# A hybrid encoder block on one core: more down-projection pairs by seven products, block sums through GpSimd's queue, and weights tiled on the host

## The chip, the cores and the metric

The kernel runs on one core of a Trainium2 chip. The metric is the device time of one execution in microseconds. TensorE is called PE, VectorE DVE, ScalarE ACT, GpSimd POOL and SyncE SP, as in the profile; a DMA's queue is called by the engine that issues it.

## What is computed

One layer of an encoder on 256 tokens of width 2048, all in float32. The reference, cut to its main lines:

```python
hn = rmsnorm(h, mix_norm_pre)
z, xbc, dt_raw, u = split(hn @ w_in)            # 2048 -> 1024 + 1536 + 32 + 1024
y_ssd = ssd_mixer(z, xbc, dt_raw, ...)          # bidirectional state-space mixer
y_pool = pool_mixer(u, pool_w, pool_scale)
h = h + rmsnorm(concat([y_ssd, y_pool]) @ w_out, mix_norm_post)
hn = rmsnorm(h, ffn_norm_pre)
gate, val = split(hn @ w_up)                    # 2048 -> 2 x 5632
ff = (gelu(dwconv_centred(gate, conv_w, conv_b)) * val) @ w_down    # 5632 -> 2048
h = h + rmsnorm(ff, ffn_norm_post)
gate = sigmoid(rmsnorm(h, ple_norm_pre) @ w_ple_gate)
h = h + rmsnorm(gate * (p @ w_ple), ple_norm_post)
```

## The kernel before

The work is a row of matmul stages on PE: "dtu" and "xbc" and "z" (parts of `w_in`), "wo" (`w_out`), "up" (`w_ffn_up`), "down" (`w_ffn_down`, names with `dn`), "ple" and "gate" (names with `gt`). Weights come from HBM into a tile called raw (three buffers of 128 x 2048 floats, 1 MiB each). A float32 product is made of three products of a shorter form: `split` (L141) lets ACT round a weight to its high part (L152) and DVE take the difference as its low part (L153), and PE adds high x high, high x low and low x high. High and low parts have five buffers each. Everything else that is large lies in 13 "pages" of 1 MiB, and intermediate results in three "mid" tiles of half that size.

**Up** (L874 to L895) goes through 11 slabs of 512 gate and 512 value columns. A slab has four calls of `feature_pairs` (L340) with two pieces each, so up has 88 pieces; a piece uses one raw tile of 8 blocks of 128 rows by 256 columns. After a slab's gate, DVE and ACT do the convolution and the gelu, POOL multiplies by `rfb`, the tokens' norm factor (L885), and after each half of the values DVE writes the activations `hid` into pages (L895). At the end of each piece `aside` (L196) runs the jobs that stand in the list `work` for that piece.

**Down** (L954, through `sublayer` and `token_major`) makes its 2048 columns in two halves of 1024. Each half goes over the 44 blocks of `hid` in 22 pairs of blocks, numbered 0 to 21. A plain pair is 2 blocks x 2 token tiles x 2 column blocks x 3 = 24 matmuls of 512 columns. A fast pair treats the 2 x 2 blocks of weights and activations by seven products instead of eight, 21 matmuls (`seven_products`, L239), and needs sums of the weights' four blocks and of the activations' four blocks. `combine` (L269) puts the products together at the end of the fast pairs of a half.

- The sums of weights are made during up by jobs of `block_sums` (L208): fetch the pair's 1 MiB into a page, add on DVE two pieces later (`add_blocks`, L232), and in the piece after that store the page to a tile in HBM. Down then loads this page again (`dn..t`) and, of the original weights, three of the four blocks (L245, L246). The last two pairs of the list are held in their pages. All these DMAs stand in SP's queue.
- The sums of activations are made in down by `pair_sums` (L773, L777 to L782), on DVE and ACT. For four of the fast pairs they are kept in two pages from the first half for the second (`dn_keep`).

The instructions are put in order per engine by a scheduler that takes those that are ready in the order of the program. `tc.issue_after(i)` puts the instructions of a block that are issued on `i`'s engine behind `i`; `load` (L116) uses it to put a DMA on SP's queue behind the last weight load.

At pair 13 of the second half the residual `h` is loaded back into two pages (`back`, L937), and at pair 16 `first_gate` (L943) prepares the gate's first pair: a load, two passes by ACT over 128 x 2048 (L948, L950) and an accumulating DMA issued by POOL (L949), which makes the low part.

In z, the mixer's output y is summed by POOL and DVE (`skip` L672, `mix` L676).

Of the kernel before, what the change touches and what calls it, by code (L numbers as in the profile page):

```python
# [11 lines left out]
F32 = mybir.dt.float32  # L12
F32R = mybir.dt.float32r
AF = mybir.ActivationFunctionType
ALU = mybir.AluOpType
# [36 lines left out]
def build(nc, a, out):  # L52
    x = a["x"][0]
    w_in, w_out, w_up = a["w_in"][0], a["w_out"][0], a["w_ffn_up"][0]
    w_down, w_gate, w_ple = a["w_ffn_down"][0], a["w_ple_gate"][0], a["w_ple"][0]
    out = out[0]

    with tile.TileContext(nc) as tc, \
# [37 lines left out]
        c_dt = DSSD + 1536  # L96
        r0 = wp.tile([P, 2048], F32, tag="raw", bufs=3, name="dtur0")
        for n in range(2):
            first = ins(nc.scalar.dma_start(r0[:, n * 352:(n + 1) * 352],
                                            w_in[:P, c_dt + n * 352:c_dt + (n + 1) * 352]))  # L100
# [15 lines left out]
        def load(dst, src, ahead=False):  # L116

            with tc.issue_after(last["dma"]) if last and not ahead else nullcontext():
                return ins(nc.sync.dma_start(dst, src))

# [35 lines left out]
        def raw(name, src, a_, b_):  # L156
            r = wp.tile([P, 2048], F32, tag="raw", bufs=3, name=name)
            if src is None:
                return r
            last["dma"] = load(r[:, :a_ * b_].rearrange("p (a b) -> p a b", a=a_), src, True)  # L160
            return r
# [46 lines left out]
        def block_sums(name, w, c0, k, held):  # L208
# [15 lines left out]
            def store():  # L224
                if not held:
                    t = dp.tile([P, 2048], F32, tag=f"{name}s{c0}_{k}", bufs=1, name=f"{name}s{c0}_{k}")
                    load(t, pg[0])
                    sums_[name, c0, k] = t, False

            return [fetch], [], [add], [store]  # L230

        def add_blocks(r):  # L232

            v = r.rearrange("p (b c) -> p b c", b=4)
            nc.vector.tensor_add(v[:, 0:2], v[:, 0:2], v[:, 1::2])  # L235
            nc.vector.tensor_add(v[:, 3], v[:, 3], v[:, 0])
            nc.vector.tensor_add(v[:, 2], v[:, 2], v[:, 3])

        def seven_products(name, stage, w, k0, c0, a_, acc, alt, start, stop):  # L239
# [3 lines left out]
            if (stage, c0, k0) in sums_:  # L243
                r = raw(f"{name}r", None, 0, 0)
                last["dma"] = load(r[:, 512:1536], w[(k0 + 1) * P:(k0 + 2) * P, c0:c0 + 1024], True)  # L245
                last["dma"] = load(r[:, :512], w[k0 * P:(k0 + 1) * P, c0:c0 + 512], True)  # L246
# [4 lines left out]
                b11 = split(f"{name}a", r[:, :512], 512)  # L251
                b2 = split(f"{name}b", r[:, 512:1536], 1024)
            else:
                r = t = raw(f"{name}r", w[k0 * P:(k0 + 2) * P, c0:c0 + 1024]
                            .rearrange("(k p) c -> p k c", p=P), 2, 1024)
                b11 = split(f"{name}a", r[:, :512], 512)
                b2 = split(f"{name}b", r[:, 1024:], 1024)
# [33 lines left out]
        def token_major(name, w, c0, ks, get, acc, tail=1, fast=(), alt=None, sums=None, at=()):  # L291
# [3 lines left out]
            for u in range(nu):  # L295
# [3 lines left out]
                if u in fast:  # L299
                    if u == fast[0]:  # L300
# [3 lines left out]
                r = None if f"{name}{k0}_0" in ready else raw(f"{name}r{k0}", w[k0 * P:(k0 + 2) * P, c0:c0 + 1024]  # L304
                                                               .rearrange("(k p) c -> p k c", p=P), 2, 1024)
# [8 lines left out]
                for t, (o, c), (k, wh, wl), q in order:  # L314
                    xh, xl = (v[:, t * P:(t + 1) * P] for v in get(k))
                    xx, ww = ((xh, wh), (xh, wl), (xl, wh))[q]
                    mm(o, xx, ww[:, c:c + o.shape[-1]], k == ks[0] and q == 0, k == ks[-1] and q == 2)
# [5 lines left out]
        def feature_major(name, w, c0, get, acc):  # L323

            for u in range(4):
                r = raw(f"{name}r{u}", w[u * 512:(u + 1) * 512, c0:c0 + 512]
                        .rearrange("(k p) c -> p k c", p=P), 4, 512)
# [12 lines left out]
        def feature_pairs(name, w, c0, get, acc):  # L340


            for u in range(2):
                r = raw(f"{name}r{u}", w[u * 1024:(u + 1) * 1024, c0:c0 + 256]
                        .rearrange("(k p) c -> p k c", p=P), 8, 256)
# [97 lines left out]
        for u in range(0, NK, 2):  # L443
            r = [wp.tile([P, 2048], F32, tag="raw", bufs=3, name=f"dtur{u}") if u else r0, page(f"dtur{u + 1}")]
            for j in range(2):
                k = u + j
                if k == 0:
                    last["dma"] = load(r[0][:, 704:1056], w_in[:P, c_dt + 704:c_dt + 1056])
# [3 lines left out]
                for c0, c1 in ((0, 704), (704, 1056)) if k == 1 else ((0, 1056),):  # L452
                    last["dma"] = load(r[j][:, c0:c1], w_in[k * P:(k + 1) * P, c_dt + c0:c_dt + c1])
# [29 lines left out]
        with tc.issue_after(half[0]), tc.issue_after(half[1]):  # L483
# [11 lines left out]
            for a_ in range(4):  # L495
# [17 lines left out]
        load(pmat.rearrange("p (g s t) -> p g s t", g=4, s=2),  # L513
             a["pool_matrix"].rearrange("g (s p) t -> p g s t", p=P))
        poolw = page("poolw")
        load(poolw.rearrange("p (g c d) -> p g c d", g=4, c=2),
             a["pool_w"][0].rearrange("g (c p) d -> p g c d", p=P))
# [122 lines left out]
        def xbc(slab):  # L640
            acc = main(f"xbc{slab}")
            feature_major(f"xb{slab}", w_in, DSSD + slab * 512, hn, acc)
# [29 lines left out]
        def skip(t):  # L672
            nc.gpsimd.tensor_tensor(by_head(y[:, t * 1024:(t + 1) * 1024]), by_head(xs[:, t * 1024:(t + 1) * 1024]),
                                    dsk.unsqueeze(2).to_broadcast([P, H, 64]), op=ALU.mult)

        def mix(t, g):  # L676
# [8 lines left out]
            nc.gpsimd.tensor_add(y[:, c0:c0 + 512], y[:, c0:c0 + 512], tm)  # L685
# [45 lines left out]
        token_major("z", w_in, 0, list(range(NK)), hn, zacc)  # L731
# [42 lines left out]
        def pair_sums(name, s, o, a11, a21, a12, a22):  # L774

            s1, s2, s3, s4 = (s[:, i * P:(i + 1) * P] for i in range(4))
# [5 lines left out]
            nc.vector.tensor_sub(o[:, 512:], s[:, :512], o[:, :512].bitcast(F32))  # L782
            return {f"s{i + 1}": (o[:, i * P:(i + 1) * P], o[:, 512 + i * P:512 + (i + 1) * P]) for i in range(4)}
# [81 lines left out]
        dn_fast, gt_fast, dn_keep = ((2, 3, 5, 7, 8, 10, 12, 13, 15, 16, 18, 19), (2, 3, 5, 7, 8, 10, 12, 13, 15, 16, 18, 19)), ((4, 6), (1, 2)), (3, 8, 13, 18)  # L865
# [7 lines left out]
        hid = []  # L873
        for s in range(DFF // 512):  # L874
            sc = mid(f"gr{s}")
            for i in range(2):
                ga = main(f"ga{s}{i}")
                feature_pairs(f"ug{s}{i}", w_up, s * 512 + i * 256, hf, ga)
# [6 lines left out]
            nc.gpsimd.tensor_tensor(cv.rearrange("p (f t) -> p f t", f=4), cv.rearrange("p (f t) -> p f t", f=4),  # L885
                                    rfb.unsqueeze(1).to_broadcast([P, 4, L]), op=ALU.mult)
            for i in range(2):
                va = main(f"va{s}{i}")
                feature_pairs(f"uv{s}{i}", w_up, DFF + s * 512 + i * 256, hf, va)
# [9 lines left out]
        def get_hid(k):  # L899
            if k % 2 == 0:  # L900
                t = lp.tile([P, 1024], F32R, tag="hs", bufs=2, name=f"hs{k}")
                src = hid[k // 8][:, (k % 8) * L:(k % 8 + 2) * L]
                nc.scalar.copy(t[:, :512], src)  # L903
                nc.vector.tensor_sub(t[:, 512:], src, t[:, :512].bitcast(F32))  # L904
# [13 lines left out]
        keep, kept = [], {}  # L918

        def hid_sums(k):  # L920


            (h1, l1), (h2, l2) = get_hid(k), get_hid(k + 1)
            if k not in kept:
                src = hid[k // 8][:, (k % 8) * L:(k % 8 + 2) * L]
                n = dn_keep.index(k // 2) if k // 2 in dn_keep else -1
                if n >= 0 and n % 2 == 0:
                    keep.append(page(f"hsum{k}", F32R))
# [150 lines left out]
```

## Time and profile before

| | us |
|---|---|
| median of 3 runs (1122.84 to 1123.28) | 1123.27 |
| the profiled execution, its own time | 1123.11 |
| its span in the profile | 1121.3 |
| up, from about 311 to 789 | 478 |
| down, from 788.96 to 1016.74 | 227.8 |
| PE busy | 1109.1 |
| DVE busy | 925.2 |
| ACT busy | 663.9 |
| POOL busy | 76.2 |

All times in the profile count from the span's start; the execution's own time has 1.8 us more around the span. DMA moved 300.87 MB in 145996 packets, nearly all of them in SP's queue; 98560 of the packets were under 2 KB and 137856 under 8 KB, since rows of a raw tile in up are 1 KB pieces of a matrix's rows, and 4 KB pieces in down. The table by stage shows busy time of each engine, granted clock, share of DMA's time and GB/s; the chain of waits shows, from the last instruction back, what each step waited for.

### The profile page before, as it was taken

The page shows a single profiled execution, that of the slowest core. Times are in us where ns is not written, and L with a number is a line of the kernel's source. Part 1 is how long each engine was busy: PE and PEld are TensorE (multiplying, and loading weights), DVE is VectorE, ACT ScalarE, POOL GpSimd, SP SyncE. Part 2 cuts the span into 40 slices and gives each one's busy share as a digit, 9 for nine tenths or more (in the row PEclk, how much of TensorE's full clock was granted, in tenths as well). Part 3 has the DMA queues.
Part 4 walks back from the last instruction along what each step waited for, and adds up shares of the span by engine and source line. Part 5 has one row for each costly group of instructions (what it writes and reads, how often), then busy time and mean ns, then how long its engine had stood idle before and what let it go on. Part 6 is the DMA issues. An engine that isn't in the chain of part 4 may idle for free.

```text
span 1121.3 us, 15775 instructions
## 1 busy us (share of the span) xinstructions
PE 1109.1 (99%) x5971; PEld 956.4 (85%) x5971; DVE 925.2 (83%) x1275; ACT 663.9 (59%) x927; POOL 76.2 (7%) x86
## 2 busy tenths in 40 slices
PE   9999999999999999999999999999999999999996
PEld 9999987888888888888888888888888888888875
DVE  6569895799898877877877768888899999889795
ACT  6847663555764554554545445445677777786672
POOL 0200004200110100000000000000000000001001
PEclk9999999999999999999999999999999999999998
DMA  9862447456789989989999898996969688995663
GB/s 363 310 207 96 170 161 269 151 188 190 252 308 347 328 300 336 314 289 309 333 330 314 276 330 289 325 304 224 339 185 334 221 286 301 383 318 177 230 235 109
DMA packets 145996, 300.87 MB, mean 268 GB/s; under 512 B 5504, under 2 KB 98560, under 8 KB 137856
## 3 DMA queue, kind: packets, MB, share of 16 engines
q1 hardware_dynamic: 145360, 298.45, 78.6%
q0 software_dynamic: 272, 1.05, 0.5%
q8 instruction: 47, 0.77, 0.3%
q10 hardware_dynamic: 288, 0.36, 0.1%
q14 instruction: 29, 0.24, 0.1%
HBM read 268.38 MB, written 31.46 MB: 267 GB/s over the span
## 4 chain that ended last, share of the span: by engine, by line
PE 96%; ACT 1%; DVE 1%; issue 1%; POOL 1%; POOLq 0%; DVEq 0%; ACTq 0%
PE va L87 22%; PE ga L87 21%; PE dna L87 14%; PE woa L87 7%; PE xbc L87 6%; PE gt L87 5%; PE dtu L87 4%; PE z L87 4%; PE dns L87 3%; PE dn0s L87 1%; PE dn1s L87 1%; PE ple L87 1%; PE pw L87 1%; PE yd L87 0%; PE gts L87 0%
## 5 line engine op out<-in xcount | busy, mean ns | idle before, releaser
L87 PE MATMUL ga<-wox,ug_0h 128*128 128x512 f32 x352 | 125.5, 395 | 0.0
L87 PE MATMUL ga<-wox,ug_1h 128*128 128x512 f32 x352 | 125.1, 394 | 0.0
L87 PE MATMUL va<-wox,uv_1h 128*128 128x512 f32 x352 | 124.8, 393 | 0.0
L87 PE MATMUL va<-wox,uv_0h 128*128 128x512 f32 x352 | 124.8, 393 | 0.0
L87 PE MATMUL ga<-wox,ug_1l 128*128 128x256 f32 x352 | 99.1, 282 | 0.0
L87 PE MATMUL ga<-wox,ug_0l 128*128 128x256 f32 x352 | 99.1, 282 | 0.0
L87 PE MATMUL va<-wox,uv_1l 128*128 128x256 f32 x352 | 99.1, 281 | 0.0
L87 PE MATMUL va<-wox,uv_0l 128*128 128x256 f32 x352 | 99.1, 281 | 0.0
L87 PEld LDWEIGHTS va<-wox,uv_1h 128*128 128x128 f32 x352 | 66.1, 188 | 15.0
L87 PEld LDWEIGHTS va<-wox,uv_0h 128*128 128x128 f32 x352 | 66.1, 188 | 15.0
L87 PEld LDWEIGHTS ga<-wox,ug_0h 128*128 128x128 f32 x352 | 66.1, 188 | 14.9
L87 PEld LDWEIGHTS ga<-wox,ug_1h 128*128 128x128 f32 x352 | 66.1, 188 | 14.9
L87 PEld LDWEIGHTS ga<-wox,ug_0l 128*128 128x128 f32 x352 | 66.2, 188 | 0.1
L87 PEld LDWEIGHTS ga<-wox,ug_1l 128*128 128x128 f32 x352 | 66.2, 188 | 0.0
L87 PEld LDWEIGHTS va<-wox,uv_0l 128*128 128x128 f32 x352 | 66.2, 188 | 0.0
L87 PEld LDWEIGHTS va<-wox,uv_1l 128*128 128x128 f32 x352 | 66.2, 188 | 0.0
L885 POOL TENSOR_TENSOR fc<-fc,rfb 128x1024 f32<-128x1024 f32 x11 | 28.0, 2547 | 438.6 <-ACT fc L884 438.6
L87 PE MATMUL dna<-dn_0h,hs 128*128 128x512 f32 x160 | 50.1, 393 | 0.0
L87 PE MATMUL dna<-dn_1h,hs 128*128 128x512 f32 x160 | 49.9, 393 | 0.0
L235 DVE TENSOR_TENSOR dnb<-dnb 128x1024 f32<-128x1024 f32 x24 | 30.8, 1283 | 17.8 <-DMA dnb<-w_ffn_down 17.6
L903 ACT CAST hs<-hid 128x512 fp32r<-128x512 f32 x44 | 27.2, 617 | 23.2 <-PE dna L87 14.8
L904 DVE TENSOR_TENSOR hs<-hid,hs 128x512 fp32r<-128x512 f32 x44 | 30.2, 686 | 9.8 <-ACT hs L903 9.7
(1903 smaller groups left out, 3105.3 us busy)
## 6 DMA issues: line engine op xcount, KB each, us to landing
dnb<-w_ffn_down SPq DMA_DIRECT2D x24, 1024.0 KB, 10.4
dns<-dnb SPq DMA_DIRECT2D x22, 1024.0 KB, 7.4
dn0r<-w_ffn_down SPq DMA_DIRECT2D x10, 1024.0 KB, 6.0
dn1r<-w_ffn_down SPq DMA_DIRECT2D x10, 1024.0 KB, 7.1
zr<-w_in SPq DMA_DIRECT2D x8, 1024.0 KB, 5.1
dtur<-w_in SPq DMA_DIRECT2D x14, 528.0 KB, 8.7
wo0r<-w_out SPq DMA_DIRECT2D x7, 1024.0 KB, 5.6
wo1r<-w_out SPq DMA_DIRECT2D x6, 1024.0 KB, 5.5
```

The source lines that it names most:

```text
L87: last["pe"] = ins(nc.tensor.matmul(o, lhsT, rhs, start=start, stop=stop, skip_group_check=True))
L235: nc.vector.tensor_add(v[:, 0:2], v[:, 0:2], v[:, 1::2])
L885: nc.gpsimd.tensor_tensor(cv.rearrange("p (f t) -> p f t", f=4), cv.rearrange("p (f t) -> p f t", f=4), rfb.unsqueeze(1).to_broadcast([P, ...
L903: nc.scalar.copy(t[:, :512], src)
L904: nc.vector.tensor_sub(t[:, 512:], src, t[:, :512].bitcast(F32))
```

## The change

Seven things are changed at once.

1. **Weights laid out on the host.** Every weight matrix is handed in as tiles: each raw tile, page or dtu block is one contiguous region with 8192 bytes a partition (4224 in dtu). For matrices that are used in pairs the first two column blocks of a pair's first row block are swapped, so that the three blocks that a fast pair needs lie side by side and come in one DMA of 6144 bytes a partition.
2. **Fast pairs.** In each half of down 14 pairs of 22 go by seven products, not 12. The order of the products and of the splits within a fast pair is changed: a, b, then the two pages of sums in the other order.
3. **Sums of activations.** For eight of the 14 pairs (`dn_stored`) they are made in up, as jobs, and stored to HBM by POOL's queue, and in both halves loaded back by POOL's queue into a mid tile. The other six are made in down in both halves. Nothing is kept in pages.
4. **Block sums.** Fetches and stores are issued by POOL (`load_aside`), the addition is three pieces after the fetch instead of two, a block sum begins every 2.5 pieces instead of 3, and there are 32 of them instead of 28. `add_blocks` is four additions of 512 columns instead of one of 1024 and two of 512.
5. **From POOL to DVE:** the product with `rfb` in up, and `skip` and the first sum of `mix` in z.
6. `back` stands at pair 20 instead of 13, and the gate's first pair at 21 instead of 16.
7. The plain products pick the swapped column block by its new place.

The diff's core:

```diff
+        def load_aside(dst, src, ahead=True):
+            with tc.issue_after(last["dma"]) if not ahead else nullcontext():
+                return ins(nc.gpsimd.dma_start(dst, src))
...
             def fetch():
                 r = page(f"{name}b{c0}_{k}")
                 pg.append(r)
-                load(r.rearrange("p (k c) -> p k c", k=2),
-                     w[k * P:(k + 2) * P, c0:c0 + 1024].rearrange("(k p) c -> p k c", p=P))
+                load_aside(r, w[c0 // 1024, k // 2], False)
...
-                    load(t, pg[0])
+                    load_aside(t, pg[0])
...
-            return [fetch], [], [add], [store]
+            return [fetch], [], [], [add], [store]
...
-            nc.vector.tensor_add(v[:, 0:2], v[:, 0:2], v[:, 1::2])
-            nc.vector.tensor_add(v[:, 3], v[:, 3], v[:, 0])
-            nc.vector.tensor_add(v[:, 2], v[:, 2], v[:, 3])
+            for i, j in ((1, 0), (0, 3), (3, 1), (2, 3)):
+                nc.vector.tensor_add(v[:, i], v[:, i], v[:, j])
...
-                last["dma"] = load(r[:, 512:1536], w[(k0 + 1) * P:(k0 + 2) * P, c0:c0 + 1024], True)
-                last["dma"] = load(r[:, :512], w[k0 * P:(k0 + 1) * P, c0:c0 + 512], True)
+                last["dma"] = load(r[:, 512:], w[c0 // 1024, k0 // 2][:, 512:], True)
...
-            t13 = split(f"{name}c", t[:, :1024], 1024)
             t42 = split(f"{name}d", t[:, 1024:], 1024)
-                    ("a11", b11, 0, alt[0], True), ("a12", b2, 0, acc[0][0], False), ("s4", b2, 512, acc[0][1], False),
-                    ("s1", t13, 0, alt[1], True), ("s3", t13, 512, alt[2], True), ("a22", t42, 0, acc[1][0], False),
-                    ("s2", t42, 512, alt[3], True)):
+            t31 = split(f"{name}c", t[:, :1024], 1024)
+                    ("a11", b11, 0, alt[0], True), ("a12", b2, 0, acc[0][0], False), ("a22", t42, 0, acc[1][0], False),
+                    ("s4", b2, 512, acc[0][1], False), ("s2", t42, 512, alt[3], True), ("s1", t31, 512, alt[1], True),
+                    ("s3", t31, 0, alt[2], True)):
...
         def skip(t):
-            nc.gpsimd.tensor_tensor(by_head(y[:, t * 1024:(t + 1) * 1024]), by_head(xs[:, t * 1024:(t + 1) * 1024]),
+            nc.vector.tensor_tensor(by_head(y[:, t * 1024:(t + 1) * 1024]), by_head(xs[:, t * 1024:(t + 1) * 1024]),
...
-            nc.gpsimd.tensor_add(y[:, c0:c0 + 512], y[:, c0:c0 + 512], tm)
+            nc.vector.tensor_add(y[:, c0:c0 + 512], y[:, c0:c0 + 512], tm)
...
-        dn_fast, gt_fast, dn_keep = ((2, 3, 5, 7, 8, 10, 12, 13, 15, 16, 18, 19), (2, 3, 5, 7, 8, 10, 12, 13, 15, 16, 18, 19)), ((4, 6), (1, 2)), (3, 8, 13, 18)
+        dn_fast, gt_fast = ((2, 3, 4, 5, 7, 8, 9, 11, 12, 13, 15, 16, 18, 19), (2, 3, 4, 5, 7, 8, 9, 11, 12, 13, 15, 16, 18, 19)), ((4, 6), (1, 2))
+        dn_stored = (2, 3, 5, 8, 11, 13, 16, 19)
...
-                work[3 * i + 2 + j].extend(jobs)
+                work[5 * i // 2 + 3 + j].extend(jobs)
...
+        def hid_sums_jobs(k):
+            o = []
+            def make():
+                o.append(lp.tile([P, 1024], F32R, tag="hs", bufs=2, name=f"he{k}"))
+                hid_sums_of(k, o[0][:, 512:].bitcast(F32), o[0])
+            def store():
+                kept[k] = dp.tile([P, 1024], F32, tag=f"hsum{k}", bufs=1, name=f"hsum{k}")
+                load_aside(kept[k], o[0].bitcast(F32))
+            return [make], [store]
+        for u in dn_stored:
+            for j, jobs in enumerate(hid_sums_jobs(2 * u)):
+                work[u // 2 * 8 + u % 2 * 2 + 6 + j].extend(jobs)
...
-            nc.gpsimd.tensor_tensor(cv.rearrange("p (f t) -> p f t", f=4), cv.rearrange("p (f t) -> p f t", f=4),
+            nc.vector.tensor_tensor(cv.rearrange("p (f t) -> p f t", f=4), cv.rearrange("p (f t) -> p f t", f=4),
...
+            o = mid(f"hd{k}", F32R)
+            if k in kept:
+                load_aside(o.bitcast(F32), kept[k])
+                d = sums_in(o)
+            else:
+                d = hid_sums_of(k, sp.tile([P, 512], F32, tag="junk", bufs=1, name=f"hs{k}"), o)
...
-                      fast=dn_fast, sums=hid_sums, at={13: back, 16: first_gate})
+                      fast=dn_fast, sums=hid_sums, at={20: back, 21: first})
...
+    def tiles(w, nk, nc):
+        k, c = w.shape
+        return w.reshape(k // P // nk, nk, P, c // nc, nc).transpose(3, 0, 2, 1, 4).reshape(c // nc, k // P // nk, P, nk * nc)
+    def pairs(w):
+        r = tiles(w, 2, 1024)
+        return np.concatenate([r[..., 512:1024], r[..., :512], r[..., 1024:]], axis=-1)
```

More of the change, by code (lines that the diff above doesn't have):

```diff
@@ L154, in split, with raw @@
             return hi, lo
-        def raw(name, src, a_, b_):
+        def raw(name, src=None):
             r = wp.tile([P, 2048], F32, tag="raw", bufs=3, name=name)
-            if src is None:
-                return r
-            last["dma"] = load(r[:, :a_ * b_].rearrange("p (a b) -> p a b", a=a_), src, True)
+            if src is not None:
+                last["dma"] = load(r, src, True)
             return r
@@ L447, in build @@
                 if k == 0:
-                    last["dma"] = load(r[0][:, 704:1056], w_in[:P, c_dt + 704:c_dt + 1056])
+                    last["dma"] = load(r[0][:, 704:1056], w_dtu[0][:, 704:1056])
                     xload(1, 2)
@@ L452, in build @@
                 for c0, c1 in ((0, 704), (704, 1056)) if k == 1 else ((0, 1056),):
-                    last["dma"] = load(r[j][:, c0:c1], w_in[k * P:(k + 1) * P, c_dt + c0:c_dt + c1])
+                    last["dma"] = load(r[j][:, c0:c1], w_dtu[k][:, c0:c1])
                 if k == 1:
@@ L941, in back, with first @@
                 last["dma"] = load(h[t], h_kept[t])
-        def first_gate():
+        def first():
             r, hi, lo = page("gtf"), page("gtfh", F32R), page("gtfl", F32R)
-            src = w_gate[:2 * P, :1024].rearrange("(k p) c -> p k c", p=P)
-            last["dma"] = load(r.rearrange("p (k c) -> p k c", k=2), src)
+            last["dma"] = load(r, w_gate[0, 0])
             nc.scalar.activation(lo, r, AF.Copy, scale=-1.0)
-            nc.gpsimd.dma_start(lo.rearrange("p (k c) -> p k c", k=2), src, accum_op=ALU.add)
+            nc.gpsimd.dma_start(lo, w_gate[0, 0], accum_op=ALU.add)
             nc.scalar.copy(hi, r)
```

89 lines of the change are left out of this document (43 added, 46 removed).

## The prediction

> **What bounds the kernel now.** I read the page's engine line and its clock and DMA slices first, then the chain of waits over the down stage, then the table by stage, and last the DMA rows and the DMA queues' own waits.
>
> ```profile
> PE 1109.1 (99%) x5971; PEld 956.4 (85%) x5971; DVE 925.2 (83%) x1275; ACT 663.9 (59%) x927; POOL 76.2 (7%) x86
> ...
> PEclk9999999999999999999999999999999999999998
> DMA  9862447456789989989999898996969688995663
> ...
> PE 96%; ACT 1%; DVE 1%; issue 1%; POOL 1%; POOLq 0%; DVEq 0%; ACTq 0%
> ```
>
> TensorE (PE) is busy for 99% of the span at full clock and is 96% of the chain. But matmul ends are modelled, so "busy" alone doesn't say that it runs at its pace. The chain in order of time does (start, length, what):
>
> ```profile
> 809.05 0.70 PE dn0s L87 x3
> 809.75 5.55 PE dna L87 x24
> 815.30 0.69 PE dns L87 x3
> ```
>
> A plain pair of the down stage is 24 matmuls in 5.55 us, a product of the seven is 3 in 0.69: both 231 ns a matmul. Two halves of 12 fast pairs (12 x 21 matmuls) and 10 plain ones (10 x 24) make 984 x 0.2312 = 227.5 us; down runs from 788.96 to 1016.74, 227.8 us. Up is 22.33 us per 128 matmuls in every piece of the chain. So both stages stand on PE's pace with no stall worth naming, though DMA and VectorE (DVE) are nearly full:
>
> ```profile
> 310.00:789.00 479.00, 479.00 (x2747) 420.38 (x2746) 386.99 (x492) 241.51 (x321) 28.37 (x12) 1.00 0.93 308
> 900.00:1010.00 110.00, 109.95 (x477) 89.05 (x476) 100.32 (x137) 81.91 (x105) 1.87 (x3) 1.00 0.92 329
> 960.00:970.00 10.00, 10.00 (x45) 8.15 (x44) 8.87 (x14) 6.82 (x10) 0.00 (x0) 1.00 1.02 415
> ```
>
> (Columns: window, length, busy PE, PEld, DVE, ACT, POOL, clock, DMA share, GB/s.) Hence only two things can shorten the run: fewer matmuls, or one of the few places where PE does wait.
>
> **The change, part by part.** The sum is made against the profiled execution's own 1123.11 us (span 1121.3, 1.8 around it); the median of the runs, 1123.27, is 0.16 above it, inside their spread.
>
> *14 fast pairs for 12.* Two pairs per half go from 24 matmuls to 21: 2 x 2 x 3 = 12 matmuls x 0.231 = **-2.8 us**, on the path, since PE has nothing beside it.
>
> *What each fast pair asks of DVE and ACT.* A fast pair splits 512 + 3 x 1024 columns: on DVE 0.68 + 3 x 1.22 = 4.34 us, a plain one 2 x 1.22 = 2.44, each plus 0.69 for the activations (L904). A computed sum of activations costs DVE 4 x 0.285 + 0.68 = 1.82 (L777 to L782). Before, per half: 12 x 4.34 + 10 x 2.44 + 22 x 0.69 = 91.7, and sums 12 x 1.82 = 21.9 in the first half, 14.6 in the second: 113.6 and 106.3. After: 14 x 4.34 + 8 x 2.44 + 15.1 = 95.4, plus only 6 x 1.82 = 10.9 (eight are made in up): 106.3 in both halves, against 112.3 us of PE. Combine and evacuation, 7.6, are the same. The half that ran without a stall before was the heavier one, so DVE holds: 0 us.
>
> *Up pays for that.* DVE gains four block sums (1.22 + 2 x 0.69, 2.6 each, in rows that nothing disturbs: 10.4), eight activation sums (14.6), and the product with rfb that leaves GpSimd (POOL), 11 x 1.22 = 13.4. It loses something too:
>
> ```profile
> L153 DVE TENSOR_TENSOR uv_1l<-uv21r,uv_1h x2: 1225/1596/1968, 413.1 to 418.6; 128x1024 fp32r<-128x1024 f32 x2
> 417.13 2.39 POOL L885 TENSOR_TENSOR fc<-fc,rfb 128x1024 f32<-128x1024 f32 x1 [41.81 <-ACT fc L884]
> ```
>
> The split at 418.6 took 1.97 us beside POOL's product, its twin 1.22. Over up, the 14 DVE instructions that run beside one of POOL's products took 15.7 us more than the medians of their forms. So DVE goes from 387 to 387 + 38.4 - 15.7 = 410 of 479 us, 86%: hidden, 0 us. The Trainium skill's page "SBUF — State Buffer", section "SBUF: two separate sides", says that DVE and GpSimd share one port pair, locked for a whole instruction, and that a DVE operation with two SBUF inputs is blocked by a GpSimd one; the rows agree. By that rule alone up to 28 us (all of L885) would come back instead of 15.7, which would only widen the cover.
>
> *y's sums go from POOL to DVE.* In z, PE's chain passes through POOL: 185.68 DVE ym 0.70, 186.45 POOL y 2.19, 188.66 DVE y 0.70, 189.41 PE yd. PE's matmuls there come 0.25 and 0.49 us later than their pace. DVE adds 128x512 in 0.69, so the link is 1.5 us shorter and both gaps go: **-0.7 us**. DVE's new work in z, 2 x 1.22 + 4 x 0.69, meets 10 us of idle in 23.
>
> *Later loads of h and the first gate pair.* In the second half ACT's two 1.9 us passes over the gate's first pair (L948, L950) come at pair 16, beside fast pairs, and PE then waits for ACT's dn132dh: 0.3 us over its pace at 987.6. At 21 they stand among plain pairs, where ACT has 2.7 of 5.55 us: **-0.3 us**. What is late next is the accumulating DMA of that pair: it took 14.4 us from issue to landing. The load ahead of it should issue with the weights of pair 20, whose counterparts issued 23 to 25 us before down's end. About 11 us for four pages, 1.9 for ACT and 14.4 end 3 to 4 us after down's end; the gate starts 6.3 after it. Hidden, by 2 or 3 us; without that cover, up to 5 us are lost.
>
> *Block sums by POOL's queue, added a piece (5.6 us) later.* This takes off SP's queue the stores that hold weights back:
>
> ```profile
> SPq L119 <- DVE dnb L237: 46.7, 14, 7.0
> DVE dnb L235 <- DMA dnb<-w_ffn_down: 17.6, 11, 3.7
> ```
>
> But the weights behind them came in time for PE all the same, so I count 0. New on POOL: some 32 fetches, 38 stores, 16 reloads, 1.43 us each to issue by its one row (L949), far below 10% of it. Behind a fetch that waits for a page stand later fetches and the small norm steps (L367); in up only the first of these matter.
>
> *Host tiles.* 1024-byte packets took 50 ns, 4096 ones 202, 8192 ones 328 (means over the run): 326, 324 and 400 GB/s on 16 engines. Weights now come in 8192-byte rows (6144 for a fast pair's rest, taken as equal). Up has 4 more fetches and stores and 8 half pages: 12.6 MB more on 148, and 161 MB in 479 us is 336 GB/s, 84% of 400 where it was 93%. No PE wait in up was a DMA's, so 0 us; it pays for the rest.
>
> Sum: 1123.1 - 2.8 - 0.7 - 0.3 = 1119.3; to set it beside the median I say **1119.4 us**.
>
> **The rivals.**
>
> *DMA becomes the bound in down's second half (slower).* A fast pair loads 0.75 + 1 MiB, a plain one 1, a stored activation sum 0.5. Second half before: 12 x 1.75 + 10 + 4 (h, gate) = 35 MiB; after: 14 x 1.75 + 8 + 8 x 0.5 + 4 = 40.5 MiB, 42.5 MB in 112.3 us: 378 GB/s. At the 317 ns that 8192-byte packets took from 900 to 1010 (413 GB/s, and 341 for the 4096-byte rows of the sums), that is 92.7 + 12.3 = 105 us: 93%, as full as now (0.92). It decides from 344 ns a packet, the mean that up shows, where 112.8 us are needed; each further 10 ns adds 3 us, so with 375 ns the half takes 122 us and the run 1129. For it: 1.02 of DMA from 960 to 970. Against: that window moved 415 GB/s and PE didn't wait. The Trainium skill's page "DMA: Bandwidth & Descriptors", section "Specifications", gives about 358 GB/s as HBM's share of a core; by it the half would take 118.7 us and the run 1125.8. The 415 GB/s here speak against it, so it gets no more than this rival's chance: **0.13**.
>
> *DVE waits for fetches in up (slower).* DVE's room in up is 69 us over 32 adds, 2.2 us each. Now 28 adds waited 17.6 + 9.7 us for DMA, 1.0 each. If POOL's DMAs land 14 us after issue and not 10, the extra piece covers it; if not, at 3 us each PE loses 27 us: 1146. Chance **0.07**.
>
> *The order isn't what it says, or the seams give it back (same).* The fetch is put behind SP's last load, but that ordering binds only instructions of SP's own engine, so on POOL free pages set when it goes. Two early fetches (2.9 us) ahead of rf0m at 307.3, which PE's rfbp waits for, give 1122.3; a late gate pair up to 1124. Chance **0.17**.
>
> The Trainium skill's page "DMA: Bandwidth & Descriptors", section "Rules for kernel authors", says that spreading DMAs over SP, ACT and GpSimd gains no bandwidth, only issue time; that is the 0 us counted above for the queue.
>
> **How the numbers follow.** Forecast 1119.4 (1117.3 with a further 2 us of seams, to 1121.0): **0.63**. Runs agree within about 0.2% (2.2 us), which is what a measurement can tell from no change: faster means under 1121.0. The range 1117.3 to 1128 takes in forecast, the seams and half of the DMA rival. Faster 0.63, same 0.17, slower 0.20.
>
> **What would show it.** Right: down some 224.7 us long with 972 matmuls of 231 ns, up still 22.33 us per 128, DMA under 0.9 in up, DVE near 410 there, L885 on DVE at 1.2 us. Wrong: gaps between products of pairs 2 to 13 of the second half ended by a DMA, DVE idle before the block sums over 69 us, a late rfbp or gtfl.

## The result and the profile after

The changed kernel takes 1129.62 us (median of 8 runs, 1125.72 to 1133.06) against 1123.30 us before (8 runs, 1122.84 to 1123.61): 1.0055 of the time before, interval 1.0038 to 1.0071. It is slower, outside the range of 1117.3 to 1128. The profiled execution took 1128.67 us, with a span of 1126.9. Of the eight runs the three slowest (1130.26 to 1133.06) are the three whose mean granted clock of PE was 0.996; the others have 0.997 or 0.998.

From the page of the changed kernel: the engines, the chain's shares by engine, the additions of block sums (count, busy us, mean ns, idle time ahead of them) and their fetches (KB, median us to landing).

```profile
PE 1107.9 (98%) x5959; PEld 954.0 (85%) x5959; DVE 936.9 (83%) x1347; ACT 668.3 (59%) x935; POOL 77.6 (7%) x155
...
PE 53%; DMA 8%; DVE 8%; issue 2%; ACT 1%; POOL 0%; DVEq 0%; POOLq 0%; ACTq 0%
...
L238 DVE TENSOR_TENSOR dnb<-dnb 128x512 f32<-128x512 f32 x112 | 75.5, 684 | 37.5 <-DMA dnb<-w_down 37.0
...
dnb<-w_down POOLq DMA_DIRECT2D x28, 1024.0 KB, 14.2
```

PE's 12 matmuls are gone (5959 for 5971), yet the chain, which was 96% PE, now runs through DMAs and DVE as well. (It reaches back only to 306.8 us, so its shares add up to some 73% of the span and not to 100%.) A fetch of block sums lands 14.2 us after its issue (10.4 before), and DVE stands 37.0 us ahead of the additions (17.6 before). Waits in up (total us, times, longest):

```profile
POOL dns L123 <- DVE dnb L238: 221.6, 25, 30.3
...
DVE dnb L238 <- DMA dnb<-w_down: 37.0, 10, 8.4
```

To place the loss I went through all matmuls in order of their ends and took from each step PE's pace, 232 ns per 512 columns; what is over is lateness, put down to the stage of the matmul that was late. "Early" is all that comes before up; "down" has also the transposes and the products of `ple` that stand between down and the gate or among the gate's first matmuls; the last column is the time from the last matmul to the span's end. For every kernel that was run, one profiled execution each, us:

| kernel | median of the runs | early | up | down | gate | after PE |
|---|---|---|---|---|---|---|
| before | 1123.3 | 23.9 | 4.1 | 1.1 | 0.5 | 8.8 |
| changed | 1129.6 | 23.6 | 9.2 | 3.2 | 0.6 | 10.2 |
| sp_both | 1122.6 | 23.8 | 4.5 | 3.1 | 0.7 | 8.9 |
| sp_fetch | 1127.7 | 23.8 | 8.5 | 3.0 | 0.7 | 9.2 |
| held_adds | 1123.9 | 23.5 | 3.9 | 3.5 | 0.7 | 10.2 |
| gate_early | 1131.5 | 23.7 | 11.0 | 5.5 | 0.3 | 10.2 |
| no_gate_first | 1125.9 | 23.4 | 4.4 | 4.9 | 2.6 | 8.9 |
| h_early | 1123.5 | 23.5 | 4.4 | 3.8 | 0.7 | 8.9 |
| apart | 1121.2 | 23.7 | 4.3 | 1.9 | 0.6 | 8.9 |
| h_early_apart | 1126.9 | 23.7 | 4.4 | 8.5 | 0.4 | 8.9 |
| late_gate | 1124.4 | 23.7 | 4.4 | 2.0 | 3.3 | 8.9 |
| comb_late | 1122.6 | 24.0 | 4.4 | 3.1 | 0.7 | 8.9 |
| apart_comb_late | 1121.4 | 23.8 | 4.4 | 1.9 | 0.6 | 8.9 |
| apart_comb_late_gate | 1123.3 | 24.3 | 4.4 | 1.8 | 2.5 | 8.9 |
| order_first | 1121.3 | 23.8 | 4.5 | 2.1 | 0.4 | 8.9 |
| apart_order | 1121.3 | 23.8 | 4.4 | 2.0 | 0.4 | 8.9 |
| pool_order | 1122.0 | 23.6 | 3.9 | 2.1 | 0.4 | 10.2 |
| swap | 1124.9 | 23.8 | 4.5 | 5.0 | 1.0 | 8.9 |
| swap_held | 1134.7 | 23.5 | 14.0 | 5.3 | 1.0 | 8.9 |
| swap_apart_held | 1132.4 | 23.6 | 15.6 | 0.9 | 1.8 | 8.9 |

The changed kernel against the one before: -2.8 (matmuls) - 0.4 (early) + 5.2 (up) + 2.1 (down) + 0.1 (gate) + 1.4 (after PE) = +5.6 (from unrounded columns), the whole difference of the two profiled executions. The medians differ by 0.8 us more, which one execution of each can't place.

One of up's waits, as the changed kernel's chain shows it (start, length, what):

```profile
445.43 0.69 DVE dnb L238
...
446.41 0.46 POOL dns L123
...
446.93 17.90 DMA dnb<-w_down
...
464.85 0.04 DVE dnb L238
...
466.81 1.14 DVE uv_0l L157
...
468.00 2.00 PE va L88 x10
```

Read it upward. PE waits for the split `uv_0l`, which DVE begins 2 us after an addition; the addition's fetch took 17.9 us; it was issued late because it stood in POOL's queue behind a store, which waited for an earlier addition. DVE had been free for the addition since 456.5 and stood 8.3 us at it, with the split queued behind. PE lost 2.0 us here.

In down the chain at the end of the second half reads:

```profile
1005.59 0.70 DVE dn1v L276
...
1006.38 0.64 DVE dn1v L278
...
1007.59 1.23 DVE dn_0l L157
...
1008.86 4.89 PE dna L88 x20
```

Operations of `combine` stand ahead of pair 20's split `dn_0l`, 1.25 us late for PE; 0.36 and 0.89 us follow at pair 21. Before the change both splits came ahead of combine.

### The profile page after: what moved, and what is told of

It reads as the page before. It is cut to its first block, busy times and chain, and to the rows that moved or that the text cites. A ratio compares the mean times of both kernels' runs of the same rounds, so it can differ in the third digit from the quotient of the medians.

```text
span 1126.9 us, 15882 instructions
## 1 busy us (share of the span) xinstructions
PE 1107.9 (98%) x5959; PEld 954.0 (85%) x5959; DVE 936.9 (83%) x1347; ACT 668.3 (59%) x935; POOL 77.6 (7%) x155
## 3 DMA queue, kind: packets, MB, share of 16 engines
q0 software_dynamic: 12528, 78.65, 17.9%
## 4 chain that ended last, share of the span: by engine, by line
PE 53%; DMA 8%; DVE 8%; issue 2%; ACT 1%; POOL 0%; DVEq 0%; POOLq 0%; ACTq 0%
PE va L88 14%; PE dna L88 13%; PE ga L88 12%; PE gt L88 5%; DMA dnb<-w_down 4%; PE dns L88 3%; PE dn0s L88 2%; PE dn1s L88 2%; DMA uv40r<-w_up 1%; DVE dnb L238 1%; DMA ug30r<-w_up 1%; DMA uv50r<-w_up 1%; DVE ug_1l L157 1%; DVE uv_1l L157 1%; DMA uv20r<-w_up 1%
## 5 line engine op out<-in xcount | busy, mean ns | idle before, releaser
L238 DVE TENSOR_TENSOR dnb<-dnb 128x512 f32<-128x512 f32 x112 | 75.5, 684 | 37.5 <-DMA dnb<-w_down 37.0
L419 ACT ACTIVATE fc<-gr,vt 128x256 f32<-128x256 f32 x44 | 24.2, 595 | 63.8 <-DVE gr L907 63.8
L88 PE MATMUL dna<-dn_1h,hs 128*128 128x512 f32 x128 | 40.6, 393 | 0.0
L88 PE MATMUL dna<-dn_0h,hs 128*128 128x512 f32 x128 | 39.8, 394 | 0.1
## 6 DMA issues: line engine op xcount, KB each, us to landing
dnb<-w_down POOLq DMA_DIRECT2D x28, 1024.0 KB, 14.2
```

Of the source, the lines that this page charges most:

```text
L88: last["pe"] = ins(nc.tensor.matmul(o, lhsT, rhs, start=start, stop=stop, skip_group_check=True))
L238: nc.vector.tensor_add(v[:, i], v[:, i], v[:, j])
L419: nc.scalar.activation(o, i, AF.Identity, bias=vec(bcol + f), scale=vec(wcol + half * wstep + f))
```

## The experiments

### Who issues, and where the additions stand

sp_both:

```diff
-                load_aside(r, w[c0 // 1024, k // 2], False)
+                load(r, w[c0 // 1024, k // 2])
...
-                    load_aside(t, pg[0])
+                    load(t, pg[0])
```

> The changed kernel with the fetches and stores of block sums issued by SP again, behind the last weight load; everything else as in the changed kernel. Four theories stand beside each other for the 6.3 us that the changed kernel lost on the median, of which the profiled executions show +5.2 in up, +2.1 in down beside the 2.8 saved, and +1.4 after the last matmul. Theory W: on POOL's queue the fetches go out in bursts, land 14 to 18 us after issue, and VectorE, whose queue is in order, stands in front of an addition for up to 8.4 us at a time. Then up's +5.2 goes, VectorE's waits for the fetches fall from 37 us to under 20, and the run comes to 1123 to 1125. Theory D: VectorE simply has too much to do in up (eight activation sums, four block sums, the product with rfb). Then the queue matters little and the run stays at 1128 to 1131. Theory S (the gate's first pair at pair 21): the 2.1 us at the end of down stay in either case. Theory Q: the time after the last matmul grew because POOL waits at the end of the program in step with the DMAs it issued; with 54 of some 70 gone, its last wait falls from 7.8 us to about 2 and the tail is back at 8.9 us.

Measured: 1122.63 us (1122.24 to 1122.87), 0.9993 of before (0.9984 to 1.0001). Up's 5.2 us are gone but for 0.4, and DVE waits for no fetch at all. DVE did the same work: its row in the table by stage (window, length, busy PE, PEld, DVE, ACT, POOL, clock, DMA share, GB/s) is

```profile
310.00:789.00 479.00, 479.00 (x2744) 419.60 (x2744) 405.74 (x577) 240.31 (x326) 5.81 (x11) 1.00 0.90 339
```

405.7 us of DVE fit into up without a stall: theory D falls. The 2 us in down stay (S). The run is a little faster than W had it, since the tail came back as well (Q): of POOL's 87 DMAs 25 remain.

sp_fetch is the first line of that diff alone.

> The changed kernel with only the fetches of block sums on SP's queue, behind the last weight load; the stores stay on POOL's. Theory W has two versions. If it is the fetch's place that hurts (a free page, not the piece, sets when POOL issues it, and it waits in POOL's queue behind stores that wait for an addition), the run is as with both on SP or better, since the stores no longer hold weights back on SP: 1122 to 1125. If it is that POOL's DMAs are slower in themselves, the stores that remain would hold pages longer and about half of the loss stays: 1126. Theory D: 1128 to 1131. Theory Q: some 42 of POOL's DMAs remain, so its last wait is about 4.5 us and the tail 9 to 9.5.

Measured: 1127.67 us (1.0026 to 1.005 of before): neither number of W; D's is nearer. But its waits are W's:

```profile
DVE dnb L238 <- DMA dnb<-w_down: 52.8, 18, 5.9
```

A fetch lands 9.2 us after issue here, sooner than with both on SP (11.2), and DVE waits more. So it isn't a slow landing as such: it is how long after the issue DVE reaches the addition. I took that lag from the traces, from the issue of each of the 32 fetches to the end of DVE's instruction ahead of its first addition: with both on SP 9.1 us at the least and 16.1 in the middle, with landings of 13.9 at most; here 4.4 and 8.2; in the changed kernel 1.1 to 50.7, with landings of 5.5 to 22.7.

held_adds keeps every DMA on POOL:

```diff
-                add_blocks(pg[0])
+                with tc.issue_after(last["dve"]): add_blocks(pg[0])
```

> The changed kernel with each block sum's additions put on VectorE behind the last split of the piece where the program has them; all DMAs stay on POOL. Theory W (the waits come from where the addition stands in VectorE's queue against the landing): the additions move back by up to a piece, VectorE's waits for fetches fall from 37 us to under 15, up loses 1 to 2 us and not 5.2, and the run comes to 1124.5 to 1126.5. Theory D: the additions then stand closer together and ahead of more splits, so PE waits as long or longer: 1129 to 1132. Theory S: the 2.1 us in down stay. Theory Q: the tail stays at 10.2 us.

Measured: 1123.88 us (1123.6 to 1124.79), just under W's range. No addition waits, though fetches still land as late as 27.2 us after issue: the lag is now 19.3 us or more. Up is at 3.9, the tail at 10.2. So W is shown from both sides, by queue and by order.

How long may a single wait be? I took all waits ahead of an addition in the traces of before, changed and sp_fetch, and PE's lateness in the 6 us after each. Of 35 up to 4.3 us two cost PE anything: one of 2.0 at 315.6, behind which stood `rfbw`, which PE's rfbp waited for (1.4 us), and one of 1.4 that came 10 us after one of 8.4 (0.3). Of five from 4.4 to 5 us two did (0.9 and 0.2), of five over 5 us four, 1.0 to 2.2 us each. In the changed kernel these losses come to 5.0 us, all but 0.2 of up's 5.2.

### The gate's first pair, the residual and combine

gate_early puts the two where they were: `at={13: back, 16: first}`.

> The changed kernel with the residual's load back at pair 13 and the gate's first pair at pair 16, as before the change. Theory S (at pair 21 ScalarE's two 1.9 us passes meet combine and PE waits 2.4 us at the end of down): those gaps go, the 0.3 us at pair 16 comes back, and the run is 1.5 to 2.1 us shorter, 1127.5 to 1128.1. Its rival, that the end of down is late because 14 fast pairs leave VectorE and ScalarE behind by themselves: the gaps only move and the run stays within 0.7 us of the changed kernel's 1129.6. Up and the tail stay as in the changed kernel in either case.

Measured: 1131.46 us (1128.1 to 1133.65). The medians of this kernel and the changed one can't be told apart, since the runs of each spread over 5 to 7 us, but the forecast gain is not there: theory S in that form fails, and in the profiled executions down is 2.3 us worse. (Of up's 11.0 us 1.6 is a stretch at half clock, see the last section.) From 978 to 1009 PE waits in eight places for splits. Four, 1.7 us together, come at pair 16, whose first split stood behind ScalarE's two passes (985.5 to 989.2). Behind the longest, 0.9 us at pair 18, is a load that took 17.8 us to land (wait: us, times, longest):

```profile
ACT dn136dh L156 <- DMA dn136t<-dns: 3.6, 1, 3.6
```

DMA is at 0.96 of its time from 900 to 1000, with 4 MiB more among the fast pairs than in the changed kernel (0.94). The next runs stand on sp_both. no_gate_first drops `21: first`; h_early sets `at={1: back, 21: first}`; apart moves the second half's last fast pairs:

```diff
-        dn_fast, gt_fast = (..., (2, 3, 4, 5, 7, 8, 9, 11, 12, 13, 15, 16, 18, 19)), ((4, 6), (1, 2))
+        dn_fast, gt_fast = (..., (2, 3, 4, 5, 7, 8, 9, 11, 12, 13, 15, 16, 17, 18)), ((4, 6), (1, 2))
-        dn_stored = (2, 3, 5, 8, 11, 13, 16, 19)
+        dn_stored = (2, 3, 5, 8, 11, 13, 16, 18)
```

> Block sums on SP's queue as in the run of 1122.6 us, and nothing prepared for the gate: its first pair is loaded and split like any other. The end of down has 2.5 us of PE waits (1.25, 0.36 and 0.89) in that run. Theory S1: ScalarE's two passes of 1.9 us and the gate's load stand ahead of pair 21's split; without them the last two waits (1.25 us together) go, and the first, in which VectorE's combine stands ahead of pair 20's split, stays. Theory S2: the residual's 2 MiB, queued ahead of pair 20's weights (which took 12.9 us to land), make everything after late; then all three stay about as they are. Theory S3: combine itself, by its place; as S2. The gate then starts with a load and a split that nothing prepared: PE may wait up to 2 us there, so the run is 1121.4 to 1124 by S1, 1122.6 to 1124.6 by S2 and S3.

Measured: 1125.92 us. Pair 21's two waits go and the 1.25 us at pair 20 stays, as S1 says; but the transposes after down and the gate's start then lose some 5 us, more than I allowed; some 1.7 of them are a stretch at half clock that follows these waits (1027.0 to 1030.4). The prepared pair earns its place.

> Block sums on SP's queue, and the residual loaded back at pair 1 of the second half, where the first half's DMA share was 0.82 and not 0.95; the gate's first pair stays at pair 21. Theory S2: pair 20's weights then land 4 to 5 us earlier, its split goes ahead of combine as it did before the change, the 2.5 us of waits shrink to under 1 and the run comes to 1120.3 to 1121.3. Theories S1 and S3: the waits stay and the run is 1122.2 to 1123. A mishap that would show: two pages less for the sums of weights in the second half, with PE waiting for a dn..t page.

Measured: 1123.52 us, in neither range. The 2.5 us at the end shrink to 0.7, as S2 says, but 2 us of new waits come at pairs 7 to 14 (914 to 954), where two pages are now taken and the chain shows `dn14t` late: the price moved.

> Block sums on SP's queue, and the last two fast pairs of the second half at 17 and 18 and not 18 and 19, so that combine runs a pair earlier, at pair 19, and the gate's first pair and the residual stay at 21 and 20. Theory S3 (combine's 8 operations of VectorE, 0.69 us each, meet the splits of pairs 20 and 21 that come late): the waits shrink to under 1 us and the run comes to 1120.3 to 1121.3. Theories S1 and S2: the waits at pairs 20 and 21 stay at 1.2 us or more, 1121.8 to 1123.

Measured: 1121.23 us (1120.78 to 1121.64), 0.9982 of before (0.9973 to 0.9991): faster than both kernels. The waits shrink by half, to 0.37 and 0.88 us; S3 has a part, not all.

> Both edits: the residual back at pair 1 and the last fast pairs at 17 and 18, with block sums on SP's queue. If S2 and S3 are two halves of one cause, this run alone has no wait at the end of down and comes to 1119.9 to 1120.6 (1122.6 less the 2.5 us of waits); if one of them is the cause alone, it is no faster than the run with that edit by more than 0.3 us. By S1 alone it stays at 1121.4 or above.

Measured: 1126.91 us, against the forecast: the waits of h_early and new ones at pairs 18 to 21 together. The two edits aren't halves of one cause.

late_gate, comb_late and their combinations on apart. The first puts `first` behind pair 21's splits, the second defers the call of combine:

```diff
+                if u == nu - 1 and "end" in at: at["end"]()
...
-                    combine(name, acc, alt, nu - tail == u + 1 and tail > 1)
+                    later.append(lambda: combine(name, acc, alt, False))
```

> Block sums on SP's queue (1122.6 us), and the gate's first pair (load, two passes, accumulating DMA) put in the program behind the splits of pair 21 instead of ahead of its load. By S1 (the passes and the load stand ahead of pair 21's split) the 0.36 and 0.89 us waits of pair 21 go while the gate keeps its prepared pair, for which 13 us were to spare: 1121.2 to 1121.6. By S3 (VectorE's order: combine ahead of the late splits) the waits stay near 2.5 us: 1122.3 to 1123. If the accumulating DMA becomes late at the gate, the gate shows a wait of its own.

Measured: 1124.37 us. Pair 21's waits are gone (S1), and ScalarE's passes now stand ahead of the gate's panel:

```profile
PEld gt L88 <- ACT dnxh L193: 2.7, 2, 1.9
```

> Block sums on SP's queue (1122.6 us), fast pairs to 19 as in the change, and combine of the down stage put behind the splits of the next pair in the program. By S3 as a matter of order (VectorE is in order, and combine's operations, some of which wait for PE, stand ahead of splits that PE needs), the waits at pairs 20 and 21 shrink from 2.5 us to under 1: 1120.6 to 1121.6. Against it: pair 21's split comes late by its load (landed at 1004.0), and combine behind it would then make PE wait for the accumulators instead, 1.5 us or more: 1122.6 to 1124.

Measured: 1122.64 us, no change, but this is no answer: DVE's order in the trace is the old one. The scheduler takes what is ready, so moving a call in the program moved nothing.

> The same order of combine with the last fast pairs of the second half at 17 and 18 (1121.2 us without it, with waits of 0.37 and 0.88 us left, in which VectorE stood 0.7 us at combine's last operation with pair 20's split behind it, whose high part had been ready for 5 us). Here nothing is late by a load, so by S3 those 1.25 us go: 1119.9 to 1120.5. If it stays within 0.3 us of 1121.2, the order isn't the cause of what was left.

Measured: 1121.37 us, for the same reason as before.

> As the run with combine behind the next splits and the last fast pairs at 17 and 18, and the gate's first pair behind the splits of pair 21 as well. By S3 the gate's pair has no part any more: within 0.3 us of that run. By S1 it is a further 0.5 to 1.2 us shorter. It would be the fastest of all at 1119.5 to 1120.2 if both hold.

Measured: 1123.34 us; late_gate's price again (1.8 us at `dnxh`).

order_first and apart_order put the order by hand. In the first, all of combine's DVE operations come behind the first split of pair 20; in the second, on apart, the four that touch PE's accumulators do.

```diff
+                    if j == 0: mark = last["dve"]
...
+                    with tc.issue_after(mark) if name[:2] == "dn" else nullcontext():
                         combine(name, acc, alt, nu - tail == u + 1 and tail > 1)
```

> Block sums on SP's queue (1122.6 us), fast pairs to 19, and combine's operations on VectorE held behind the first split of pair 20, so that the order there really is split, split, combine. By S3 (order) the first wait of 1.25 us goes, the 0.36 and 0.89 us at pair 21 stay, since those come from the load and ScalarE's passes ahead of pair 21's split: 1121.2 to 1121.7. By S2 (late loads alone) pair 20's split can't run earlier and combine only comes later: 1122.4 to 1123.5.

Measured: 1121.26 us (1121.05 to 1121.53), 0.9981 of before (0.9972 to 0.999), as S3 says. Two chains of the same place, sp_both first:

```profile
1001.08 0.70 DVE dn1v L276
...
1001.87 0.65 DVE dn1v L278
...
1003.09 1.23 DVE dn_0l L157
...
1004.36 4.89 PE dna L88 x20
```

```profile
1001.71 0.70 PE dn1s L88 x3
1002.41 2.80 PE dna L88 x12
1005.21 0.02 issue
1005.23 0.04 DVE dna L277
```

In the second PE goes from its products to pair 20 without a step on DVE. The 0.36 and 0.9 us at pair 21 stay.

> Block sums on SP's queue, the last fast pairs of the second half at 17 and 18 (1121.2 us), and those four operations of combine that wait for PE's accumulators held behind the first split of pair 20. By S3 the 0.37 and 0.88 us left at pair 20 go, since that split's high part was ready 5 us before: 1119.8 to 1120.4. If combine behind the split makes PE wait for the accumulators, 1.0 us or so comes back: 1121 to 1121.6.

Measured: 1121.25 us (1120.93 to 1121.44): the forecast's second branch. The split comes early, and combine's last operation comes 0.7 us late, behind a split of activations.

pool_order is held_adds with apart_order's edits.

> All fetches and stores of block sums on POOL's queue as in the change, additions held behind the splits of their piece, the last fast pairs at 17 and 18, combine's four operations held behind the first split of pair 20. If POOL's queue costs nothing but its wait at the program's end (1.4 us more after the last matmul than with 25 DMAs), the run is the one with SP's queue plus 1.4 us: 1121.2 to 1121.8. If its DMAs hurt elsewhere as well (weights landing late beside bursts), 1122.5 or more.

Measured: 1122.03 us (1121.63 to 1122.24), 0.8 over apart_order: 1.4 more after PE, 0.5 less in up. Once the order is held, POOL's queue costs only its tail.

swap is order_first with `at={20: first, 21: back}`; swap_held adds held_adds' line, swap_apart_held apart's edit too.

> Block sums on SP's queue, combine behind pair 20's first split (1121.3 us), the gate's first pair at pair 20 and the residual at pair 21, behind that pair's weights as far as the queue goes. By S1 and S2 together (passes, and 3 MiB of loads ahead of the weights of pairs 20 and 21) pair 21's split comes 3 us earlier and the remaining 1.25 us go: 1119.8 to 1120.4. If the passes now stand ahead of pair 20's split instead, 1 us or more comes back there: 1121 to 1122. A residual that lands late would show as a wait ahead of the transposes after down.

Measured: 1124.91 us. Here PE waits 1.9 us at pair 21 for combine's last operation, which came behind that pair's second split, and 0.5 us for a split of `ple`, whose weights landed late. Right after that PE runs at half clock for 3.4 us (granted clock 0.50 from 1014 to 1016), which costs 1.5 us more.

> The same with the additions of block sums held behind the splits of their piece. VectorE already waits for no fetch there, so theory W gives no more than the 0.5 us that the held run's up was below the one with SP's queue: 0 to 0.6 us under the swap run, 1119.3 to 1120.3.

Measured: 1134.66 us, 14 over the forecast and the slowest of all, and instructive. SP's waits in up, order_first and then swap_held:

```profile
SPq L118 <- DVE dnb L238: 21.1, 8, 7.6
```

```profile
SPq L118 <- DVE dnb L238: 113.1, 18, 12.3
```

An addition that comes later keeps its store waiting, and on SP the weights stand behind that store: a load of `ug50r` was issued at 515.89, 0.9 us after a store at which SP had stood for 7.2 us until DVE had gone on; it landed at 527.66, and PE waited for it.

> The same as the run before it, with the last fast pairs of the second half at 17 and 18. Combine and the gate's pair are then at different pairs; if nothing is left to collide, it is within 0.3 us of that run, and if something is left there it is up to 1 us shorter: 1118.8 to 1120.3.

Measured: 1132.36 us; up loses as much, with 1.1 us of half clock in it, while down, at 0.9, is the best of all and the gate pays 1.4 for it against order_first.

## Why the prediction was wrong, point by point

- **14 fast pairs.** Right: 12 matmuls fewer at an unchanged pace, -2.8 us.
- **y's sums on DVE.** Right, 0.5 of the 0.7. Taken by stage, z's lateness is 7.5 us before and 7.1 in every one of the 19 kernels with the change, and in sp_both's chain z has neither DVE nor POOL. The "early" column hides this, since the lateness of the program's first stage, dtu, scatters from 5.5 to 6.4 us.
- **DVE in down and up.** Right. In down no wait lay inside the halves; in up I counted 410 us, sp_both shows 405.7 and no stall.
- **Block sums by POOL's queue, "so I count 0".** This step failed: 5.2 us in up and 1.4 after PE. I had seen in the third rival that the ordering doesn't bind on POOL, and priced only what it does at rf0m (where an addition's wait ahead of `rfbw` did cost 1.4 of the 5.2). It also lets POOL issue in bursts: 12 of the 31 steps between fetches are under 2 us, four fetches went out from 400.78 to 402.38 and landed 9.3, 13.8, 18.2 and 22.7 us later, and then none for 36 us, behind stores that waited for additions. "The extra piece covers it" holds on SP, where the lag is 16.1 us in the middle, not on POOL.
- **The rival "DVE waits for fetches"** had the mechanism, at 0.07, but sized it by an average: 2.2 us of room for each addition. 37.0 us over the 28 additions of down's sums is 1.3 each, inside that room, and PE still lost. DVE works through its queue in order, so here the single waits decided (four of five over 5 us cost PE, two of 35 up to 4.3 us), not the mean.
- **`back` and the gate's pair at 20 and 21, -0.3.** Failed with its sign: +2.1. I asked whether the accumulating DMA would be late (it wasn't: it landed at 1018.5, before the gate began) and not what pair 21 shares with combine, which runs there too. "At 21 they stand among plain pairs, where ACT has 2.7 of 5.55 us" left out the loads: 3 MiB ahead of the weights of pairs 20 and 21, and two passes ahead of a split. order_first shows that combine ahead of pair 20's split cost 1.25 us, and h_early, where the residual no longer stands ahead of that pair's weights, has 0.7 left of the 2.5; no_gate_first and late_gate show that the gate's pair cost the rest. Every other place that I tried for it cost as much or more.
- **Host tiles.** Right as far as seen: DMA in up at 0.87 to 0.90 where I had 84%, and no loss that follows from it.
- **The DMA rival.** Not in the changed kernel: 0.94 of DMA's time from 900 to 1000 and no wait of PE there. h_early (2 MiB more among the fast pairs) and pair 18 of gate_early show how near it is: loads come late at once.
- The issue of a DMA on POOL took 0.54 us, not 1.43; this changed nothing.

Against the forecast of 1119.3 for the profiled execution (1128.67) this adds up: 5.2 and 1.4 from POOL's queue, 2.4 from the two jobs at pairs 20 and 21 (+2.1 for -0.3), 0.3 less gained ahead of up, 0.1 in the gate.

What stays open: why apart, order_first and apart_order, which take away different waits, all end at 1121.2 to 1121.3. Each has 1.2 to 1.5 us left at pairs 20 and 21, at another place. Open too is why the lag halves in sp_fetch, where only the stores are on another queue than in sp_both.

## What to carry to other kernels

DVE and POOL took their queues in order here, so an operation that waits for a transfer must stand far enough behind its issue. The figure to read is each transfer's lag between issue and use against its own landing, and the longest single wait, not the mean of the waits. Comparing the shortest lag with the longest landing asks too much: with both on SP the two were 9.1 and 13.9 us, of different transfers, and nothing waited. Moving a DMA to another engine's queue also takes away the order that its old queue gave it: say by hand what must come after what, and look in the trace whether the order was taken. Here POOL's queue did well only with held additions, and SP's only without.

## What the runs showed of the hardware that was not expected

**POOL's last wait grows with the DMAs it issued.** At the program's end POOL has a DRAIN (times, ns shortest/middle/longest, first and last start), before and after the change:

```profile
L58 POOLq DRAIN  x3: 40/89/755, 1114.2 to 1121.1; - x3
```

```profile
L59 POOLq DRAIN  x3: 46/102/7774, 1118.3 to 1126.6; - x3
```

With 1, 25, 55 and 87 DMAs issued by POOL it took 0.76, 2.71, 5.16 and 7.77 us (before, sp_both, sp_fetch, changed): 0.08 us for each, though the last of them had landed 100 us earlier. It begins 1.7 us after the last matmul. With 87 it ends 1.6 us behind the landing of the last output and lengthens the run; with 55 it still ends 1.0 us ahead of that landing, so the 0.3 us of sp_fetch's tail are not its doing. The Trainium skill's page "VectorE: DVE Perf Modes", section "The DRAIN you can't avoid", gives some 12 ns, constant, for the DRAINs at a program's start and end on all five engines; for POOL's here the measurement decides otherwise. DVE's longest at the end is 2.77 us before and after. What POOL does in that time, no run shows.

**Two queues share DMA evenly.** While POOL's burst was under way (401 to 425, changed kernel), the queues of SP (q1) and POOL (q0) moved (packets, MB, share of 16 engines):

```profile
q1 hardware_dynamic: 723, 5.24, 53.5%
q0 software_dynamic: 727, 4.73, 47.1%
```

Hence POOL's 1 MiB fetches land one after another 5.0 us apart there, where loads that SP had almost to itself landed 2.5 us apart (sp_both, 991 to 1002). The Trainium skill's page "DMA: Bandwidth & Descriptors", section "Queues, rings and completion order", says that a DMA engine goes round its queues packet by packet; these rows agree. A burst on one queue thus takes half of DMA from the weights on the other, and its last fetch waits for all that stand ahead of it.

**A wait of PE can be followed by a stretch at half clock.** In five of the 20 profiled executions the granted clock was 0.5 once within the program, for 3.4 us each time: from 470.7 in gate_early, 1027.0 in no_gate_first, 1013.0 in swap, 1023.1 in swap_held and 529.3 in swap_apart_held. A matmul of 512 columns then took some 0.43 us instead of 0.23, and the stretch cost PE 1.1 to some 1.7 us. Each begins within 2.5 us of the end of a wait of PE of 1 us or more. Not every such wait has one behind it: the changed kernel's 2.0 us at 466 to 468 had none. What decides, no run here shows.
